# Neighbourhood attention: transposes of two steps issued together, values one turn later

## The chip, the cores and the metric

The kernel is one program on one core of a Trainium2 chip. The metric is the device time of one execution in microseconds (us), from the runs of the kernel before and of the changed kernel on the same chip. The engines are named as in the profile: PE (TensorE, matmuls; PEld its weight loads), DVE (VectorE), ACT (ScalarE), POOL (GpSimd), SP (SyncE, which issues DMAs).

## The reference

The reference is one layer of a hybrid encoder over 512 tokens of width 1024. After an RMS norm, one projection feeds three branches: a bidirectional mLSTM, a two-dimensional neighbourhood attention, and a cross-attention into 256 memory tokens. Each branch is projected back to width 1024, weighted by a sigmoid gate, summed, projected, and added to the input; a convolutional gated FFN and a final norm follow. The change lies in the neighbourhood attention alone (8 heads of 64, a grid of 8 rows by 64 columns, a window of 16 columns):

```python
s = jnp.einsum('bhrcd,bhrkjd->bhrckj', qg, k_band) * (NA_HEAD_DIM ** -0.5) + bias[None]
s = jnp.where(col_ok[None, None, None, :, None, :], s, -jnp.inf)
p = jax.nn.softmax(s.reshape(B, NA_HEADS, rows, GRID_W, kr * GRID_W), axis=-1).reshape(s.shape)
o = jnp.einsum('bhrckj,bhrkjd->bhrcd', p, v_band)
```

## The kernel before

Every float32 matrix product is made of three matmuls on two-part operands (`mm3`, L213 to L215: high by high, high by low, low by high). Weights come by DMA on SP's queue as raw blocks (`wr`) and are split into a high part `wh` by ACT (L195) and a low part `wl` by DVE (L196). There are four buffers each of `wh` and `wl`, so two blocks of two halves are held, and a split waits for PE to have read the block before the last.

The branches A, B and C are written as generators (`ml_all`, `na_all`, `xa_all`). The main code runs the dense projections and, between them, takes one turn of the generator at the head of a list with `step`. So PE gets a block of dense matmuls (24 of 512 columns, half of them for one output tile each where a block has two), then a few short matmuls of a branch, then the next block. The neighbourhood attention takes 18 such turns, t = 0 to 17, beside the gate projections (`gate`, drained by L1196 and L1197) and branch projections (drained by L1224 and L1225) of the second and third branch.

Its work is 16 steps i, one for each head and each half of the columns. A step has four stages:

- `scores(i)`: four matmuls of 256 columns (L944, L945) of zero-padded two-part queries (`QS`, `QZ`) with keys (`KS`) into one PSUM bank. DVE adds the bias and finds the maximum (L949), negates it (L951), ACT takes the exponential with row sums (L954), DVE the reciprocal (L955), ACT scales (L957). The result is the tile `sm`, shown as `s`.
- `transposes(i)`: four 128x128 transposes of `sm` on PE (L963) into one bank; ACT makes the high part (L970) and DVE the low part (L971) of two weight tiles `w`.
- `values(i)`: four matmuls of 256 columns (L982) of `w` with a window of values `vw`.
- `store(i)`: ACT and DVE add the parts and split the result (L994 to L1003) into `yh` and `yl`, which the third branch's projection reads after the last turn.

In turn t the kernel before issues `scores(t)`, then `values(t - 2)` and `store(t - 2)`, then `transposes(t - 1)`. `prep` (L920 to L924) makes queries and keys of the next pair of heads; it is called after the scores of turns 3, 7 and 11, and its instructions stand, as the scheduler placed them, in the odd turns. It writes the low part of the queries into `QZ`, of which there are two sets of two tiles, cleared once by POOL (L909). `load_vwin` issues 32 small DMAs on POOL's queue for the value window of a pair of heads, four steps ahead of its use.

A scheduler (the Tile layer) sets each engine's order from the order of the code, the free buffers and its own cost model; each engine then runs its list strictly in that order and waits at semaphores. The pools that matter here: four PSUM banks for scores, transposes and values (`at`), four for the dense products (`mm`), seven scratch tiles `s`, two `E` tiles for `w`, four `H` tiles.

Of the kernel before, what the change touches and what calls it, by code (L numbers as in the profile page):

```python
# [11 lines left out]
F32 = mybir.dt.float32  # L12
F32R = mybir.dt.float32r
# [4 lines left out]
P = 128  # L18
S = 512
# [91 lines left out]
def hybrid_block(ctx, tc, xg, xT, memT, wflat, vecs, gbias, nabias, outa, outb, outc):  # L111
    nc = tc.nc
    V, A, G, PE, SY = nc.vector, nc.scalar, nc.gpsimd, nc.tensor, nc.sync
# [5 lines left out]
    tp = ctx.enter_context(tc.tile_pool(name="tp", bufs=2))  # L119
# [6 lines left out]
    def nm(s):  # L126
        uid[0] += 1
        return f"{s}_{uid[0]}"

    def unit(dt=F32):  # L130
        return up.tile([P, UNIT], dt, tag="unit", name=nm("u"))

    def scr(n=512):
        return sp.tile([P, S], F32, tag="scr", name=nm("s"))[:, :n]

    def tiny(n):
        return tp.tile([P, 32], F32, tag="tiny", name=nm("y"), bufs=12)[:, :n]
# [4 lines left out]
    def atps():  # L142
        return atp.tile([P, 512], F32, tag="at", name=nm("at"))
# [144 lines left out]
    for i in range(2):  # L288
        t = cp.tile([P, 514], F32, name=f"pad{i}")
# [212 lines left out]
    for c in range(3):  # L502
        n, nk = TMC[c], TMK[c]
# [29 lines left out]
    def load_vwin(hp):  # L533

        vw = unit(F32R)
        for b in range(4):
            for hf in range(2):
                i = 2 * b + hf
                for r in range(4):
                    G.dma_start(vw[r * 32:(r + 1) * 32, i * 256:(i + 1) * 256],  # L540
                                nav_v[hf, r, CW[b]:CW[b] + 32, hp * 256:(hp + 1) * 256])
        return vw
# [360 lines left out]

    def na_all(nq, nk, vw0, yh, yl):

        QZ = [[tp.tile([P, S], F32R, tag="H", name=nm("QZ"), bufs=4) for _ in range(2)] for _ in range(2)]
        for pair in QZ:
            for e in range(2):
                G.memset(pair[e][64 - 64 * e:128 - 64 * e].bitcast(F32), 0.0)  # L909

        def prep(hp):
            qn = nq[:, hp * S:(hp + 1) * S]
            kn = nk[:, hp * S:(hp + 1) * S]
            QL = QZ[hp % 2]
            QS, KS = [], []
            for e in range(2):
                own, oth = slice(64 * e, 64 * e + 64), slice(64 - 64 * e, 128 - 64 * e)
                q2 = tp.tile([P, S], F32R, tag="R", name=nm("QS"), bufs=4)
                k2 = tp.tile([P, S], F32R, tag="R", name=nm("KS"), bufs=4)
                A.activation(q2[own], qn[own], AF.Copy)  # L920
                A.activation(k2[own], kn[own], AF.Copy)
                A.activation(q2[oth], qn[own], AF.Copy)
                V.tensor_tensor(k2[oth], kn[own], k2[own].bitcast(F32), op=ALU.subtract)
                V.tensor_tensor(QL[e][own], qn[own], q2[own].bitcast(F32), op=ALU.subtract)  # L924
                QS.append(q2)
                KS.append(k2.rearrange("p (r w) -> p r w", r=ROWS))
            return QS, KS, QL

        def bias_tile(i):
            bt = tp.tile([P, 2 * M], F32, tag="nab", name=nm("nab"))  # L930
            SY.dma_start(bt, nabias[i // 2, i % 2])
            return bt

        def scores(i, ops, bt):
            QS, KS, QL = ops
            e, bp = (i // 2) % 2, i % 2
            ps = atps()
            sm = scr()
            mx = tiny(2)
            for j in range(2):  # L940
                b = 2 * bp + j
                bs = slice(b * P, (b + 1) * P)
                ks = KS[e][:, :, CW[b]:CW[b] + 32]
                PE.matmul(ps[:, j * M:(j + 1) * M], QS[e][:, bs], ks, start=True, stop=False)  # L944
                PE.matmul(ps[:, j * M:(j + 1) * M], QL[e][:, bs], ks, start=False, stop=True)  # L945
            smv = sm.rearrange("p (a b) -> p a b", a=2)
            for j in range(2):
                js = slice(j * M, (j + 1) * M)
                V.tensor_tensor_reduce(smv[:, j, :], ps[:, js], bt[:, js], 1.0, 2.0 * NEG, ALU.add, ALU.max,  # L949
                                       accum_out=mx[:, j:j + 1])  # L950
            V.tensor_scalar(mx, mx, -1.0, None, op0=ALU.mult)  # L951
            su = tiny(2)
            for j in range(2):
                A.activation(smv[:, j, :], smv[:, j, :], AF.Exp, bias=mx[:, j:j + 1], accum_out=su[:, j:j + 1])  # L954
            V.reciprocal(su, su)  # L955
            for j in range(2):
                A.activation(smv[:, j, :], smv[:, j, :], AF.Copy, scale=su[:, j:j + 1])  # L957
            return sm

        def transposes(i, sm):  # L960
            pt = atps()
            for j in range(4):
                PE.transpose(pt[:, j * P:(j + 1) * P], sm[:, j * P:(j + 1) * P], ident)  # L963

            pp = []
            for bl in range(2):
                w = tp.tile([P, 4, P], F32R, tag="E", name=nm("w")).rearrange("p a b -> p (a b)")
                wv = w[:, :512].rearrange("p (k x q) -> p k x q", k=2, x=2)
                src = pt[:, bl * 256:(bl + 1) * 256].rearrange("p (k q) -> p k q", k=2)
                A.activation(wv[:, :, 0, :], src, AF.Copy)  # L970
                V.tensor_tensor(wv[:, :, 1, :], src, wv[:, :, 0, :].bitcast(F32), op=ALU.subtract)  # L971
                pp.append(w)
            return pp

        def values(i, pp, vw):

            e, bp = (i // 2) % 2, i % 2
            py = atps()
            for bl in range(2):
                for hf in range(2):  # L980
                    c = (2 * (2 * bp + bl) + hf) * 256 + e * P
                    PE.matmul(py[:, bl * 256:(bl + 1) * 256], vw[:, c:c + P], pp[bl][:, hf * 256:(hf + 1) * 256],  # L982
                              start=hf == 0, stop=hf == 1)
            return py

        def store(i, py):

            h, bp = i // 2, i % 2
            e = h % 2
            hs, es, os = slice(h // 2 * S, (h // 2 + 1) * S), slice(64 * e, 64 * e + 64), slice(64 - 64 * e, 128 - 64 * e)  # L990
            pv = py.rearrange("p (b x q) -> p b x q", b=2, x=2)
            y = scr(256)
            yv = y.rearrange("p (b q) -> p b q", b=2)
            A.activation(yv[es], pv[os, :, 0, :], AF.Copy)  # L994
            V.tensor_tensor(yv[es], yv[es], pv[es, :, 1, :], op=ALU.add)
            V.tensor_tensor(yv[es], yv[es], pv[es, :, 0, :], op=ALU.add)
            bs = slice(2 * bp, 2 * bp + 2)
            y4 = y[es].rearrange("p (b r c) -> p b r c", b=2, r=ROWS)
            yhv = yh[es, hs].rearrange("p (r b c) -> p b r c", r=ROWS, b=4)[:, bs]
            ylv = yl[es, hs].rearrange("p (r b c) -> p b r c", r=ROWS, b=4)[:, bs]  # L1000
            for b in range(2):
                A.activation(yhv[:, b], y4[:, b], AF.Copy)
                V.tensor_tensor(ylv[:, b], y4[:, b], yhv[:, b].bitcast(F32), op=ALU.subtract)  # L1003

        n = 16
        ops = prep(0)
        bt = bias_tile(0)
        sms, pts = {}, {}
        vws = {0: vw0}
        yield  # L1010
        for t in range(n + 2):
            if t < n:
                nb = bias_tile(t + 1) if t + 1 < n else None
                sms[t] = scores(t, ops, bt)
                bt = nb
                if t % 4 == 3 and t + 1 < n:
                    ops = prep((t + 1) // 4)
            i = t - 2
            if 0 <= i:
                if i % 4 == 0 and i + 4 < n:  # L1020
                    vws[i // 4 + 1] = load_vwin(i // 4 + 1)
                store(i, values(i, pts.pop(i), vws[i // 4]))
            i = t - 1
            if 0 <= i < n:
                pts[i] = transposes(i, sms.pop(i))
            yield


# [103 lines left out]
    for f in range(4):  # L1132
        ps = paced(("o", f), RN if f else RB)
        t = scr()
# [50 lines left out]
    for br in range(3):  # L1185
# [3 lines left out]
        if br == 1:  # L1189
            vw0 = load_vwin(0)  # L1190
            ys[2] = [unit(F32R), unit(F32R)]
            gens.append(na_all(nq, nk, vw0, *ys[2]))
            step(1)
# [360 lines left out]
```

## Time and profile before

| | |
|---|---|
| time, median of 3 runs | 873.18 us (872.92 to 873.79) |
| the profiled execution's own time | 873.18 us |
| its span, first to last instruction | 871.2 us |
| PE busy | 865.8 us, 99% of the span |
| DVE, ACT, POOL busy | 594.7, 467.8, 125.4 us (68%, 54%, 14%) |
| granted PE clock | 1.000 |
| turns of the neighbourhood attention | from 312.2 us to 427.5 us |

The first matmul row of a turn (L944) marks its start, and a start is more telling than a duration here: matmuls overlap in the array, a 512-column one is recorded with 0.39 us but the next starts 0.227 us later. The rows that the argument uses stand in the prediction.

### The profile page before, as it was taken

How to read it: one execution, taken by the hardware profiler on the slowest of the kernel's cores; microseconds unless marked ns; L12 is line 12 of the kernel's file. 1: busy time of each engine (PE TensorE's matmuls, PEld its weight loads, DVE VectorE, ACT ScalarE, POOL GpSimd, SP SyncE). 2: the span in 40 equal slices, each digit the busy share in tenths (PEclk: the TensorE clock that was granted, in tenths of full speed). 3: DMA queues.
4: the chain of work that ended last, by engine and by line, in shares of the span. 5: the costliest groups of instructions: out<-in, count | busy, mean ns of one | idle time of the engine just before them, and what ended most of it. 6: DMA issues, size and time to landing. Idle time of an engine off the chain costs nothing.

```text
span 871.2 us, 12230 instructions
## 1 busy us (share of the span) xinstructions
PE 865.8 (99%) x4287; PEld 733.9 (84%) x4287; DVE 594.7 (68%) x1292; ACT 467.8 (54%) x981; POOL 125.4 (14%) x202
## 2 busy tenths in 40 slices
PE   9999999999999999999999999999999999999997
PEld 7898889888888888888888888888888888888887
DVE  7794698997477768897676558776633466666534
ACT  7563577764355658897534455444422344444532
POOL 0101100000344370600000002111100011111010
PEclk9999999999999999999999999999999999999999
DMA  8324643533343453533223433323233323232412
GB/s 281 101 75 147 196 140 89 169 107 115 93 132 82 113 146 112 160 116 122 99 96 109 144 109 97 98 96 98 78 98 113 102 96 97 96 98 87 141 35 97
DMA packets 39421, 99.81 MB, mean 115 GB/s; under 512 B 5688, under 2 KB 13880, under 8 KB 39360
## 3 DMA queue, kind: packets, MB, share of 16 engines
q1 hardware_dynamic: 31568, 92.32, 32.6%
q0 software_dynamic: 7360, 6.32, 3.4%
q8 instruction: 34, 0.56, 0.3%
q10 hardware_dynamic: 432, 0.39, 0.1%
q14 instruction: 27, 0.22, 0.1%
HBM read 94.80 MB, written 4.21 MB: 114 GB/s over the span
## 4 chain that ended last, share of the span: by engine, by line
PE 98%; DVE 1%; issue 0%; ACT 0%; POOL 0%; POOLq 0%
PE mm L213 29%; PE mm L215 29%; PE mm L214 29%; PE at L214 2%; PE at L213 2%; PE at L215 2%; PE at L982 1%; PE at L963 1%; PE at L944 0%; PE at L945 0%; PE at L765 0%; PE at L813 0%; PE at L1070 0%; PE at L243 0%; PE mm L422 0%
## 5 line engine op out<-in xcount | busy, mean ns | idle before, releaser
L213 PE MATMUL mm<-u,wh 128*128 128x512 f32 (+1 forms) x1072 | 414.3, 386 | 0.0
L215 PE MATMUL mm<-u,wl 128*128 128x512 f32 (+1 forms) x1072 | 411.8, 384 | 0.0
L214 PE MATMUL mm<-u,wh 128*128 128x512 f32 (+1 forms) x1072 | 411.5, 384 | 0.0
L195 ACT ACTIVATE wh<-wr 128x512 fp32r<-128x512 f32 (+2 forms) x298 | 184.2, 621 | 219.9 <-PE mm L214 177.2
L196 DVE TENSOR_TENSOR wl<-wr,wh 128x512 fp32r<-128x512 f32 (+3 forms) x300 | 203.4, 681 | 88.5 <-ACT wh L195 86.4
L215 PEld LDWEIGHTS mm<-u,wl 128*128 128x128 f32 x1072 | 201.3, 188 | 40.3 <-DVE wl L196 0.4
L213 PEld LDWEIGHTS mm<-u,wh 128*128 128x128 f32 x1072 | 201.5, 188 | 39.0 <-ACT wh L195 0.4
L214 PEld LDWEIGHTS mm<-u,wh 128*128 128x128 f32 x1072 | 201.5, 188 | 38.5
L1418 POOL TENSOR_TENSOR s<-s,rb 128x512 f32<-128x512 f32 x22 | 38.2, 1736 | 401.7 <-DVE s L1417 238.9
L540 POOL DMA_DIRECT2D u<-nav_d x128 | 62.5, 535 | 70.5 <-DVE X L220 24.3
L219 ACT ACTIVATE u<-s 128x512 fp32r<-128x512 f32 x26 | 16.4, 632 | 56.4 <-DVE s L1421 56.3
L1421 DVE TENSOR_TENSOR s<-mm,s 128x512 f32<-128x512 f32 x22 | 15.2, 690 | 23.9 <-POOL s L1418 23.9
L460 ACT ACTIVATE s<-pad,vec 128x512 f32<-128x512 f32 x30 | 24.4, 813 | 9.7 <-DVE pad L458 9.7
L220 DVE SCALAR_TENSOR_TENSOR u<-s,u 128x512 fp32r<-128x512 f32 x26 | 19.1, 733 | 14.8 <-ACT u L219 14.5
L461 DVE SCALAR_TENSOR_TENSOR s<-pad,vec,s 128x512 f32<-128x512 f32 x30 | 22.5, 750 | 5.5 <-ACT s L460 5.5
L1417 DVE SCALAR_TENSOR_TENSOR s<-s,s 128x512 f32<-128x512 f32 x22 | 15.2, 691 | 13.4 <-ACT s L1416 13.3
L462 DVE SCALAR_TENSOR_TENSOR s<-pad,vec,s 128x512 f32<-128x512 f32 x30 | 22.5, 750 | 0.9
L1416 ACT ACTIVATE s<-s 128x512 f32<-128x512 f32 x22 | 13.9, 632 | 14.9 <-DVE s L1415 14.9
L1196 DVE TENSOR_TENSOR s<-mm,rb_x 128x512 f32<-128x512 f32 x16 | 11.0, 689 | 13.8 <-PE mm L215 13.7
L458 DVE TENSOR_TENSOR pad<-mm,rb 128x512 f32<-128x512 f32 x22 | 15.1, 690 | 6.4 <-PE mm L215 6.2
L1428 DVE TENSOR_TENSOR u<-mm,u 128x512 f32<-128x512 f32 x13 | 9.0, 692 | 14.6 <-PE mm L215 14.6
L214 PE MATMUL mm<-wl,u 128*128 128x512 f32 x48 | 18.7, 390 | 0.0
(352 smaller groups left out, 1053.3 us busy)
## 6 DMA issues: line engine op xcount, KB each, us to landing
wr<-wflat SPq DMA_DIRECT2D x141, 512.0 KB, 3.3
nab<-nabias SPq DMA_DIRECT2D x16, 256.0 KB, 2.7
u<-nav_d POOLq DMA_DIRECT2D x128, 32.0 KB, 2.8
s<-xT SPq DMA_DIRECT2D x15, 256.0 KB, 4.0
wr<-wflat SPq DMA_DIRECT2D x14, 192.0 KB, 2.4
nav_d<-nv POOLq DMA_DIRECT2D x8, 256.0 KB, 2.5
R<-rd SPq DMA_DIRECT2D x8, 256.0 KB, 4.6
wr<-wflat SPq DMA_DIRECT2D x2, 544.0 KB, 3.4
```

The lines of the kernel that those rows point to most:

```text
L195: A.activation(h[:, u:v], src, AF.Copy)
L196: V.tensor_tensor(l[:, u:v], src, h[:, u:v].bitcast(F32), op=ALU.subtract)
L213: PE.matmul(ps, lh, rh, start=start, stop=False)
L214: PE.matmul(ps, lh, rl, start=False, stop=False)
L215: st["mm"] = PE.matmul(ps, ll, rh, start=False, stop=stop).ins
L219: A.activation(h, src, AF.Copy, scale=scale)
L220: V.scalar_tensor_tensor(l, src, scale, h.bitcast(F32), op0=ALU.mult, op1=ALU.subtract)
L460: A.activation(t1, pad[:, 0:512], AF.Identity, scale=vcol(w, i), bias=vcol(b, i))
L461: V.scalar_tensor_tensor(t1, pad[:, 1:513], vcol(w, n + i), t1, op0=ALU.mult, op1=ALU.add)
L462: V.scalar_tensor_tensor(t1, pad[:, 2:514], vcol(w, 2 * n + i), t1, op0=ALU.mult, op1=ALU.add)
L540: G.dma_start(vw[r * 32:(r + 1) * 32, i * 256:(i + 1) * 256], nav_v[hf, r, CW[b]:CW[b] + 32, hp * 256:(hp + 1) * 256])
L1418: G.tensor_tensor(c, c, rb2, op=ALU.mult)
```

## The change

In turn t the changed code issues `values` and `store` of step t - 3 first, then the transposes, then `scores(t)`. Transposes are issued in odd turns only, of the two steps t - 2 and t - 1 (step 0 alone in turn 1, step 15 alone in turn 16); in turn 17 the values of steps 14 and 15 come together. The weight tiles of odd steps now have two tiles of their own (`odd`, of the pool `H`), those of even steps stay in the pool `E`. To free the two `H` tiles there is one set of zero-padded low queries (`QL`) in place of two, with half of the clearing on POOL.

```diff
-        QZ = [[tp.tile([P, S], F32R, tag="H", name=nm("QZ"), bufs=4) for _ in range(2)] for _ in range(2)]
-        for pair in QZ:
-            for e in range(2):
-                G.memset(pair[e][64 - 64 * e:128 - 64 * e].bitcast(F32), 0.0)
+        QL, odd = [[tp.tile([P, S], F32R, tag="H", name=nm(n), bufs=4) for _ in range(2)] for n in ("QZ", "w")]
+        for e in range(2):
+            G.memset(QL[e][64 - 64 * e:128 - 64 * e].bitcast(F32), 0.0)
...
-            QL = QZ[hp % 2]
...
-                w = tp.tile([P, 4, P], F32R, tag="E", name=nm("w")).rearrange("p a b -> p (a b)")
+                if i % 2:
+                    w = odd[bl]
+                else:
+                    w = tp.tile([P, 4, P], F32R, tag="E", name=nm("w")).rearrange("p a b -> p (a b)")
...
         for t in range(n + 2):
+            for i in range(max(0, t - 3), t - 2 + (t == n + 1)):
+                if i % 4 == 0 and i + 4 < n:
+                    vws[i // 4 + 1] = load_vwin(i // 4 + 1)
+                store(i, values(i, pts.pop(i), vws[i // 4]))
+            if t % 2 or t == n:
+                for i in range(max(0, t - 2 + (t == n)), t):
+                    if i in sms:
+                        pts[i] = transposes(i, sms.pop(i))
             if t < n:
                 nb = bias_tile(t + 1) if t + 1 < n else None
                 sms[t] = scores(t, ops, bt)
                 bt = nb
                 if t % 4 == 3 and t + 1 < n:
                     ops = prep((t + 1) // 4)
-            i = t - 2
-            if 0 <= i:
-                if i % 4 == 0 and i + 4 < n:
-                    vws[i // 4 + 1] = load_vwin(i // 4 + 1)
-                store(i, values(i, pts.pop(i), vws[i // 4]))
-            i = t - 1
-            if 0 <= i < n:
-                pts[i] = transposes(i, sms.pop(i))
             yield
```

The code below the change keeps its text; line numbers of the changed kernel differ by one or two (L944 becomes L942, L963 becomes L961, L982 becomes L983, L949 becomes L947, L955 becomes L953, L971 becomes L972). PE keeps the same instructions in the same number.

PE's order at turn 9, between two dense blocks (`mm` tiles), before:

```order
L215 MATMUL mm_4236<-u_149,wl_4150 128x512
L944 MATMUL at_4265<-KS_4106,QS_4105 128x256
L945 MATMUL at_4265<-KS_4106,QZ_3418 128x256
L944 MATMUL at_4265<-KS_4106,QS_4105 128x256
L945 MATMUL at_4265<-KS_4106,QZ_3418 128x256
L982 MATMUL at_4281<-w_4219,u_3623 128x256 x2
L982 MATMUL at_4281<-w_4222,u_3623 128x256 x2
L963 MATMUL at_4294<-ident,s_4186 128x128 x4
L213 MATMUL mm_4316<-u_147,wh_4228 128x512
```

The same turn in the changed kernel (`s_4178` is the softmax of step 8, `s_4093` that of step 7):

```order
L215 MATMUL mm_4204<-u_149,wl_4129 128x512
L983 MATMUL at_4231<-w_4084,u_3659 128x256 x2
L983 MATMUL at_4231<-w_4087,u_3659 128x256 x2
L961 MATMUL at_4244<-ident,s_4093 128x128 x4
L961 MATMUL at_4253<-ident,s_4178 128x128 x4
L942 MATMUL at_4266<-KS_4109,QS_4108 128x256
L943 MATMUL at_4266<-KS_4109,QZ_3418 128x256
L942 MATMUL at_4266<-KS_4109,QS_4108 128x256
L943 MATMUL at_4266<-KS_4109,QZ_3418 128x256
L213 MATMUL mm_4293<-u_147,wh_4196 128x512
```

The scores moved from the front of the group to its end, and two sets of transposes stand side by side; the even turns beside it hold only values and scores.

DVE's order in turn 8, from the first part of step 8's scores (`s_4186`) to the reciprocal of its row sums, before:

```order
L949 ISA s_4186,y_4187<-at_4185,nab_4087 128x256
L949 ISA y_4187 128x1
L1225 TENSOR_TENSOR u_2709<-u_2709,s_4049 128x512
L949 ISA s_4186,y_4187<-at_4185,nab_4087 128x256
L949 ISA y_4187 128x1
L995 TENSOR_TENSOR s_4206<-s_4206,at_4201 64x256
L951 TENSOR_SCALAR y_4187<-y_4187 128x2
L971 TENSOR_TENSOR w_4219<-at_4214,w_4219 128x2x128
L996 TENSOR_TENSOR s_4206<-s_4206,at_4201 64x256
L196 TENSOR_TENSOR wl_4229<-wr_4050,wh_4228 128x512
L955 RECIPROCAL y_4195<-y_4195 128x2
```

The same stretch in the changed kernel (step 8's scores are `s_4178`, its reciprocal the last row):

```order
L947 ISA s_4178,y_4179<-at_4177,nab_4090 128x256
L947 ISA y_4179 128x1
L997 TENSOR_TENSOR s_4167<-s_4167,at_4162 64x256
L947 ISA s_4178,y_4179<-at_4177,nab_4090 128x256
L947 ISA y_4179 128x1
L196 TENSOR_TENSOR wl_4201<-wr_3987,wh_4200 128x512
L1004 TENSOR_TENSOR u_3417<-s_4167,u_3416 64x8x16 x2
L949 TENSOR_SCALAR y_4179<-y_4179 128x2
L196 TENSOR_TENSOR wl_4286<-wr_4122,wh_4285 128x512
L953 RECIPROCAL y_4187<-y_4187 128x2
```

No low part of a transposed weight tile (L971 before) stands in this even turn any more; the store of an earlier step (L997, L1004) and two splits of dense weights (L196) stand ahead of the reciprocal, and of the splits only one comes between the negated maximum (L949 now) and the reciprocal.

## The prediction

> **What bounds the kernel now.** I read the page first, then who PE waits for, then the turns of the neighbourhood attention by windows, then single rows. The page's busy times and its chain that ended last:
>
> ```profile
> span 871.2 us, 12230 instructions
> ...
> PE 865.8 (99%) x4287; PEld 733.9 (84%) x4287; DVE 594.7 (68%) x1292; ACT 467.8 (54%) x981; POOL 125.4 (14%) x202
> ...
> PE 98%; DVE 1%; issue 0%; ACT 0%; POOL 0%; POOLq 0%
> ```
>
> PE is the chain: 98% of it. The view of waits for PE has one row in the whole execution, at the first matmul:
>
> ```profile
> PE at L243 <- PEq L1541: 0.8, 1, 0.8
> ```
>
> So in the stage of the change PE never waits, and there are two ways to another time: PE's own instructions take less or more, or something is late that was in time. Windows by turn (columns: length; busy us and instructions of PE, PEld, DVE, ACT, POOL; granted clock; DMA share; GB/s), turns 7, 8, 9 and 14:
>
> ```profile
> 358.82:365.68 6.86, 6.86 (x37) 5.90 (x36) 5.82 (x17) 6.70 (x17) 4.81 (x10) 1.00 0.58 157
> 365.68:372.55 6.87, 6.87 (x37) 5.90 (x36) 6.64 (x19) 4.77 (x14) 0.03 (x1) 1.00 0.19 51
> 372.55:379.42 6.87, 6.87 (x38) 5.90 (x36) 6.45 (x18) 6.43 (x17) 0.00 (x0) 1.00 0.62 194
> ...
> 406.88:413.75 6.87, 6.87 (x37) 5.90 (x36) 4.80 (x15) 5.09 (x15) 0.00 (x0) 1.00 0.23 78
> ```
>
> All turns last the same 6.87 us at full clock, whether DVE has 4.80 or 6.64 us of work in them. In turns 7 to 9 DVE and ACT are nearly as full as PE; that is where lateness would begin.
>
> **What PE pays for each kind of group.** PE's timeline (start, duration), turns 0, 1, 2, 4 and the end of 17:
>
> ```profile
> 312.16 0.28 PE L944 MATMUL at<-KS,QS 128*128 128x256 f32 x1
> ...
> 312.64 0.39 PE L213 MATMUL mm<-u,wh 128*128 128x512 f32 x1
> ...
> 318.08 0.28 PE L944 MATMUL at<-KS,QS 128*128 128x256 f32 x1
> ...
> 324.48 0.28 PE L944 MATMUL at<-KS,QS 128*128 128x256 f32 x1
> ...
> 338.22 0.28 PE L944 MATMUL at<-KS,QS 128*128 128x256 f32 x1
> ...
> 338.70 0.64 PE L982 MATMUL at<-w,u 128*128 128x256 f32 x4
> 339.17 0.60 PE L963 MATMUL at<-ident,s 128*128 128x128 f32 x4
> 339.53 0.48 PE L213 MATMUL mm<-u,wh 128*128 128x512 f32 x1
> 339.85 0.39 PE L214 MATMUL mm<-u,wh 128*128 128x512 f32 x1
> 340.08 0.40 PE L215 MATMUL mm<-u,wl 128*128 128x512 f32 x1
> ...
> 345.08 0.28 PE L944 MATMUL at<-KS,QS 128*128 128x256 f32 x1
> ```
>
> Turn 0 has 24 dense matmuls, from 312.64 to 318.08: 5.44 us, 0.227 each. Before them stand the four scores, 0.48 us. Turn 1 (scores, transposes, 24 dense) lasts 6.40 us against 5.92 for turn 0, so a set of four transposes costs 0.48 (0.473 before rounding of the starts). Turn 4 lasts 6.86, so a group of four values adds 0.47. The costs add up; there is no large price for changing kind.
>
> How much of the 0.473 is hand-over? One transpose is recorded with 0.272 us, four together with 0.60 (339.17):
>
> ```profile
> L963 PE MATMUL at<-ident,s x64: 270/272/276, 318.6 to 421.4; 128*128 128x128 f32 x64
> ```
>
> So three intervals take 0.60 - 0.27 = 0.33, one 0.109, and four transposes 0.437. What is left, 0.473 - 0.437 = 0.036 us, is the hand-over: the first dense matmul after them begins while the last transpose still runs and the second comes only 0.32 later (339.53 to 339.85), the third after 0.23.
>
> **The change, part by part.**
>
> *Fewer hand-overs.* The instructions of PE stay; their groups change. 16 sets of transposes become 7 pairs and 2 singles, so 7 hand-overs go: 7 x 0.036 = 0.25 us gained, all of it on the path, since PE is the path. The trace has no two sets side by side and no scores behind transposes. Bounds: if all 16 hand-overs vanish, because scores now stand between transposes and the dense block, 16 x 0.036 = 0.6 us gained; if a short score pays for the transposes the 0.09 us that the first dense matmul shows above 0.227 (0.32), in each of 9 places, 0.8 us lost. I take 0.25, nearest to the measured set.
>
> The Trainium skill, page "TensorE: Matmul & The Clock Gate", section "Back-to-back issue gap", gives for sustained pairs of weight load and matmul about 81 ns at 128 columns and about 131 ns at 512. By it a second set of four could take 0.32 instead of 0.437, an estimate of 7 x 0.11 = 0.8 us more gain, 872.2 in all. The rows disagree with the skill at the long end (0.227 measured, 0.131 stated) and show 0.109 at the short end, so the sum goes by the rows.
>
> *Values one turn later, scores last.* Nothing is added on PE. The transposes of an even step come earlier against PE's work: ahead of those of step 8 stand one group of scores (0.48) and one of values (0.47) fewer than before. This is the one place where cover shrinks. Step 8's softmax on DVE and ACT, and its transposes (turn 9):
>
> ```profile
> 369.14 0.17 DVE L951 TENSOR_SCALAR y<-y 128x2 f32<-128x2 f32 x1
> 369.34 0.42 DVE L971 TENSOR_TENSOR w<-at,w 128x256 fp32r<-128x256 f32 x1
> 369.80 0.42 DVE L996 TENSOR_TENSOR s<-s,at 64x256 f32<-64x256 f32 x1
> 370.25 0.69 DVE L196 TENSOR_TENSOR wl<-wr,wh 128x512 fp32r<-128x512 f32 x1
> 370.86 0.16 DVE L955 RECIPROCAL y<-y 128x2 f32<-128x2 f32 x1
> ...
> 369.34 0.51 ACT L954 ACTIVATE s<-s,y 128x256 f32<-128x256 f32 x1 [1.62 <-DVE y L951]
> ...
> 370.25 0.19 ACT L954 ACTIVATION_READ_ACCUMULATOR s<-s,y 128x1 f32 x1
> ...
> 371.40 0.91 ACT L957 ACTIVATE s<-s,y 128x256 f32<-128x256 f32 x2
> ...
> 373.50 0.60 PE L963 MATMUL at<-ident,s 128*128 128x128 f32 x4
> ```
>
> It is ready at 371.40 + 0.91 = 372.31, 1.19 us before PE takes it, the shortest margin of the even steps. After: PE comes at 373.50 - 0.95 - 0.11 (three hand-overs gone by then) = 372.44. DVE: from the reciprocal of step 0 to that of step 8 the changed list has two more L196 (2 x 0.69), and one each of L971, L995, L996 fewer (3 x 0.42): 0.12 more. Between L951 and the reciprocal two items fewer (L971, L996) now hide the exponentials; these need 1.3 us (from 369.14 to the end of the second read at 370.44), the one L196 left covers 0.69. So L951 comes at about 369.14 + 0.12 + 0.84 = 370.1, the reciprocal at 371.5 and the softmax at 371.5 + 0.2 + 0.91 = 372.6. PE waits about 0.15 us there. Steps 2, 6, 12 and 14 have an L1224 and L1225 or a set of L971, L995 and L996 less ahead of their reciprocals, and more margin to begin with; I put them, with 4 and 10, at no wait. What a wait holds up: everything behind it on PE, since PE takes its list in order; so it is paid in full.
>
> *Transposed weights.* Those of odd steps are read one turn after they are made, as before; the tightest place is in the second half of step 6's (DVE, then PE's second pair 0.23 behind the row's start):
>
> ```profile
> 365.75 0.41 DVE L971 TENSOR_TENSOR w<-at,w 128x256 fp32r<-128x256 f32 x1
> ...
> 366.17 0.64 PE L982 MATMUL at<-w,u 128*128 128x256 f32 x4
> ```
>
> Ready at 366.16, read at 366.40. In the changed order an even step's weights have a turn more (over 6 us); an odd step's are split first in their turn and gain the scores that now stand behind them. The added L971 of the pair lies beside PE's dense block. No cost. Weight splits (`wh`, `wl`) that slip behind the pair are covered by the two-block buffers: ACT's splits spend their time waiting for PE, not the reverse:
>
> ```profile
> L195 ACT ACTIVATE wh<-wr 128x512 fp32r<-128x512 f32 (+2 forms) x298 | 184.2, 621 | 219.9 <-PE mm L214 177.2
> ```
>
> *One query set, other queues.* The low queries are written by L924 after the same DVE list has used the scores that read them, so one set adds no wait; the two clearings that go are POOL's, of 0.52 us each and 80 us ahead of the first scores:
>
> ```profile
> L909 POOL MEMSET QZ<- x4: 518/520/523, 187.5 to 232.1; 64x512 f32 x4
> L540 POOL DMA_DIRECT2D u<-nav_d x32: 492/499/557, 346.5 to 365.2; - x32
> ```
>
> The last value window (32 DMAs, second row) waits for values of an earlier window, so it may begin a turn later, near 353, and be in by 375; its first values come in turn 15, after 406.88. SP's bias tiles swap places with a weight block, and each is issued a turn (6.4 us at least) ahead of its scores; the page shows 2.7 us to landing:
>
> ```profile
> nab<-nabias SPq DMA_DIRECT2D x16, 256.0 KB, 2.7
> ```
>
> After turn 17 two gate blocks (10.9 us of dense work) still stand before the third branch's projection and cover two stores instead of one.
>
> **Sum.** 873.18 - 0.25 + 0.15 = 873.1 us. The profiled execution's 873.18 is 1.98 more than its span and equals the median of the runs. A change of 0.2% (1.75 us) is about what a measurement of this kernel can tell from none.
>
> **Rivals.**
> - *Softmaxes late (slower).* In the odd turns DVE gets both splits of a pair and half of `prep`; turns 8 and 9 have 6.64 and 6.45 us of DVE in 6.87, so a backlog of an odd turn has nowhere to go before the next transposes. If one L196 more (0.69) comes ahead at steps 4, 8 and 10, which all lie beside or just behind branch projections, that is 2.1 us and 875.2. It decides from 2.0 us of waits in all. Against it: the DVE work ahead of each reciprocal grows by no more than 0.12 us, and the later steps (turn 14: 4.80 us) have room.
> - *Nothing saved.* The hand-over costs the same into scores, and small waits stay: 873.2 to 874.8.
> - *A real gain (faster).* It takes 1.75 us. If the second set ran at the dense pace (0.227 / 4 = 0.057 for 128 columns) instead of 0.109, 28 transposes would give 1.5 and the hand-overs 0.25: 871.4. Against it: within a set the later transposes already follow without a break, and show 0.109.
>
> **How the numbers follow.** Forecast (hand-overs saved, waits under 0.4 us): 0.62, own range 872.4 to 873.6. Nothing saved or small waits: 0.21. Softmaxes late by 2 us or more: 0.12. Real gain: 0.05. Faster 0.05, within 0.2% 0.83, slower 0.12. The range leaves out the real gain and most of the large waits, and takes in, below, both gains together (0.25 and 0.6) and the 0.3 us by which the lowest run (872.92) lies under the median, and above, two steps that wait 0.9 us each with nothing saved: 872.0 to 874.9.
>
> **What would show it.** Right: turns of the changed kernel near 6.4 us (even) and 7.3 us (odd) that sum to 13.7 per pair; eight transposes in 0.87 us; no PE wait but some 0.1 us at turn 9. Wrong: rows of PE waiting for ACT's L955 at L961 in several odd turns, for DVE at L983, or transposes closer than 0.109.

## The result: slower by 0.27%, and the profile after

The changed kernel took 875.69 us (median of 10 runs, 875.38 to 876.16), the kernel before 873.27 us (10 runs, 872.79 to 873.93) on the same chip. The ratio is 1.0027 with an interval of 1.0017 to 1.0037. The forecast was 873.1, range 872.0 to 874.9: the time lies above the range. Two executions among the experiments, one of 1245 us (*scores between*) and one of 3116 us (*tiles only*), were far slower than the others of their kernels and are left out of the medians below.

The page of the changed kernel, the lines that answer to those of before (span, busy time by engine, the chain that ended last by engine):

```profile
span 873.9 us, 12233 instructions
...
PE 867.7 (99%) x4287; PEld 733.8 (84%) x4287; DVE 595.9 (68%) x1292; ACT 467.6 (54%) x981; POOL 123.5 (14%) x200
...
PE 93%; DVE 3%; ACT 2%; issue 1%; POOL 0%; POOLq 0%; DVEq 0%
```

PE is still 99% busy by the records, but the chain is PE for 93% only. DVE and ACT together now hold 5% of it. The view of waits for PE names the place: transposes that wait for the scaling of the softmax.

```profile
PE at L961 <- ACT s L955: 0.7, 1, 0.7
```

This view shows only gaps that reach past the modelled end of the matmul before. To see all that was lost I use one stretch that holds the same instructions in every kernel: from the first scores of turn 0 to the end of the nineteen dense blocks that start there. In windows of that stretch (columns as in the prediction: length, then busy us and instructions of PE, PEld, DVE, ACT, POOL), the kernel before and the changed one:

```profile
312.16:438.36 126.20, 126.20 (x649) 107.88 (x648) 99.91 (x273) 97.97 (x247) 26.24 (x54) 1.00 0.42 128
```

```profile
312.59:441.05 128.46, 127.67 (x649) 107.79 (x648) 99.94 (x273) 97.04 (x247) 26.13 (x54) 1.00 0.42 126
```

128.46 - 126.20 = 2.26 us, of 2.42 between the medians. So nearly the whole loss is in the turns of the neighbourhood attention. Below, "the stage" is this stretch. Turns 7, 8, 9, 11 and 16 of the changed kernel:

```profile
358.23:365.81 7.58, 7.58 (x42) 6.31 (x40) 6.43 (x19) 6.62 (x16) 5.16 (x11) 1.00 0.65 165
365.81:372.21 6.40, 6.40 (x33) 5.47 (x32) 6.37 (x18) 4.37 (x13) 4.84 (x10) 1.00 0.40 99
372.21:380.62 8.41, 7.73 (x41) 6.31 (x40) 6.55 (x19) 7.56 (x20) 0.00 (x0) 1.00 0.47 152
...
387.03:394.86 7.83, 7.72 (x41) 6.30 (x40) 7.35 (x21) 6.39 (x17) 0.00 (x0) 1.00 0.22 69
...
422.41:429.19 6.78, 6.78 (x33) 5.41 (x32) 4.00 (x10) 4.19 (x11) 0.00 (x0) 1.00 0.23 77
```

Even turns last 6.40 or 6.41 us, all of them. An odd turn without a wait lasts 7.32 (turns 9 and 11 of a later experiment, *stores after the scores*, show it). Turns 7, 9 and 11 last 7.58, 8.41 and 7.83, so they wait 0.26, 1.09 and 0.51 us. Turn 16 lasts 6.78 where it takes 6.38 in the experiment *no scaling*, without a wait: 0.40 us. Turn 15, with 7.42, adds 0.1. The sum is 2.36 us of waits, and 0.10 us is gained elsewhere in the stage.

**The chain of step 8.** PE, DVE and ACT of the changed kernel in turns 7 to 9 (start, duration, idle time before it and what ended it):

```profile
361.48 0.43 DVE L972 TENSOR_TENSOR w<-at,w 128x256 fp32r<-128x256 f32 x1 [0.42 <-ACT w L971]
...
362.82 0.42 DVE L972 TENSOR_TENSOR w<-at,w 128x256 fp32r<-128x256 f32 x1 [0.26 <-ACT w L971]
...
363.97 0.41 DVE L947 CUSTOM_DVE_ANT_0 s<-at,nab 128x256 f32<-128x256 f32 x1
...
366.64 0.29 PE L943 MATMUL at<-KS,QZ 128*128 128x256 f32 x1
...
367.01 0.16 DVE L953 RECIPROCAL y<-y 128x2 f32<-128x2 f32 x1
...
368.33 0.68 DVE L196 TENSOR_TENSOR wl<-wr,wh 128x512 fp32r<-128x512 f32 x1
...
369.54 0.40 DVE L996 TENSOR_TENSOR s<-s,at 64x256 f32<-64x256 f32 x1
369.87 0.41 DVE L947 CUSTOM_DVE_ANT_0 s<-at,nab 128x256 f32<-128x256 f32 x1
...
370.89 0.68 DVE L196 TENSOR_TENSOR wl<-wr,wh 128x512 fp32r<-128x512 f32 x1
...
371.89 0.15 DVE L949 TENSOR_SCALAR y<-y 128x2 f32<-128x2 f32 x1
...
373.21 0.17 DVE L953 RECIPROCAL y<-y 128x2 f32<-128x2 f32 x1 [0.57 <-ACT s L952]
...
373.41 0.91 ACT L955 ACTIVATE s<-s,y 128x256 f32<-128x256 f32 x2 [0.23 <-DVE y L953]
...
372.69 0.60 PE L961 MATMUL at<-ident,s 128*128 128x128 f32 x4
373.97 0.84 PE L961 MATMUL at<-ident,s 128*128 128x128 f32 x4 [0.68 <-ACT s L955]
```

The scores of step 8 are done on PE at 366.93 (366.64 + 0.29). DVE touches them first at 369.87, 2.9 us later. Until then it works off other things: the drains of a branch projection, a split of weights, and L996, the store of an earlier step. Between the two parts of the bias stands L997, behind them another split and two L1004. The softmax is done at 373.41 + 0.91 = 374.32. PE is ready for it at 372.69 + 4 x 0.11 = 373.13. Already in turn 7 the same happened: the bias of step 7 begins at 363.97, behind the four splits of the pair (L972), two of which wait for ACT. In the kernel before, step 7's reciprocal stood here:

```profile
363.27 0.17 DVE L955 RECIPROCAL y<-y 128x2 f32<-128x2 f32 x1 [0.65 <-ACT s L954]
```

So step 7's reciprocal came at 363.27 before and at 367.01 now, step 8's at 370.86 and 373.21. (0.43 us of each difference is only the start of the stage, 312.59 for 312.16.)

**The wait of turn 11** has another face. DVE and ACT in turn 10:

```profile
382.96 0.42 DVE L947 CUSTOM_DVE_ANT_0 s<-at,nab 128x256 f32<-128x256 f32 x1
...
384.03 0.42 DVE L996 TENSOR_TENSOR s<-s,at 64x256 f32<-64x256 f32 x1 [0.64 <-ACT s L995]
384.49 0.43 DVE L947 CUSTOM_DVE_ANT_0 s<-at,nab 128x256 f32<-128x256 f32 x1
...
382.88 0.71 ACT L1198 ACTIVATE s<-s,mgbh 128x512 f32<-128x512 f32 x1
383.62 0.38 ACT L995 ACTIVATE s<-at 64x256 f32<-64x256 f32 x1
385.41 0.51 ACT L1003 ACTIVATE u<-s 64x128 fp32r<-64x128 f32 x2 [1.41 <-DVE s L997]
385.94 0.51 ACT L952 ACTIVATE s<-s,y 128x256 f32<-128x256 f32 x1
```

L996 belongs to the store of step 7. It stands between the two parts of step 10's bias and waits 0.64 us for ACT's L995, which stands behind the gate's tanh (L1198). The second part of the bias stands behind it and waits too. Then the store's copies (L1003) go ahead of the exponentials (L952) on ACT.

### The profile page after: what moved, and what is told of

Its sections match the earlier page's. It is cut to its first block, busy times and chain, and to the rows that moved or that the text cites. A ratio compares the mean times of both kernels' runs of the same rounds, so it can differ in the third digit from the quotient of the medians.

```text
span 873.9 us, 12233 instructions
## 1 busy us (share of the span) xinstructions
PE 867.7 (99%) x4287; PEld 733.8 (84%) x4287; DVE 595.9 (68%) x1292; ACT 467.6 (54%) x981; POOL 123.5 (14%) x200
## 4 chain that ended last, share of the span: by engine, by line
PE 93%; DVE 3%; ACT 2%; issue 1%; POOL 0%; POOLq 0%; DVEq 0%
PE mm L215 28%; PE mm L213 28%; PE mm L214 28%; PE at L214 2%; PE at L213 2%; PE at L215 2%; PE at L961 1%; PE at L983 1%; ACT s L955 1%; DVE s L947 0%; PE at L765 0%; PE at L813 0%; PE at L1071 0%; ACT s L952 0%; PE at L243 0%
## 5 line engine op out<-in xcount | busy, mean ns | idle before, releaser
L196 DVE TENSOR_TENSOR wl<-wr,wh 128x512 fp32r<-128x512 f32 (+3 forms) x300 | 204.7, 685 | 87.7 <-ACT wh L195 85.6
L952 ACT ACTIVATE s<-s,y 128x256 f32<-128x256 f32 x32 | 16.0, 501 | 9.4 <-DVE y L949 9.2
```

The source lines that it names most:

```text
L196: V.tensor_tensor(l[:, u:v], src, h[:, u:v].bitcast(F32), op=ALU.subtract)
```

## The experiments

Two theories stood at the start. A: PE comes to the transposes of an even step 0.95 us earlier, and its softmax isn't ready by then. B: the burst of work that a pair makes in one turn on DVE and ACT delays everything. C to F came with the runs and are told in their expectations. All edits are to the changed kernel unless it is said otherwise. The time of before is that of runs on the same chip.

| kernel | time, us | before, us | ratio (interval) | stage, us |
|---|---|---|---|---|
| before | 873.27 | | | 126.20 |
| changed | 875.69 | 873.27 | 1.0027 (1.0017 to 1.0037) | 128.46 |
| stores after the scores | 873.49 | 873.48 | 1.0000 (0.9991 to 1.0009) | 126.31 |
| scores first | 873.49 | 873.45 | 1.0001 (0.9992 to 1.0009) | 126.32 |
| scores between | 876.07 | 873.48 | 1.0030 (1.0018 to 1.0042) | 128.83 |
| unpaired | 876.41 | 873.45 | 1.0035 (1.0021 to 1.0048) | 129.24 |
| pairs a turn later | 873.00 | 873.36 | 0.9995 (0.9986 to 1.0004) | 126.02 |
| unpaired, a turn later | 873.42 | 873.36 | 1.0002 (0.9993 to 1.0011) | 126.31 |
| no scaling | 873.32 | 873.48 | 0.9998 (0.9989 to 1.0007) | 126.10 |
| longer softmax | 878.04 | 873.45 | 1.0051 (1.0037 to 1.0065) | 130.44 |
| adds left out | 874.13 | 873.36 | 1.0010 (1.0001 to 1.0019) | 127.27 |
| adds on POOL | 876.59 | 873.45 | 1.0031 (1.0020 to 1.0043) | 129.64 |
| tiles only (on before) | 873.23 | 873.36 | 0.9999 (0.9989 to 1.0008) | |

### Which part of the change costs: order or pairing

*Scores first*: the pairs and the later values stay, the scores go back to the front of their turn.

```diff
         for t in range(n + 2):
+            if t < n:
+                ... scores(t) and prep, as below
             for i in range(max(0, t - 3), t - 2 + (t == n + 1)):
                 store(i, values(i, pts.pop(i), vws[i // 4]))
             if t % 2 or t == n:
                 ... transposes
-            if t < n:
-                ... scores(t) and prep
```

> The changed kernel with the scores at the front of each turn again (scores of t, values of t-3, then the pair of transposes); pairs, tiles and values a turn later stay. Theory A (the even step's transposes came 0.95 us earlier against its softmax, and PE waits for that): the waits of turns 7 to 16, 2.6 us in the changed kernel, go but for 0.3 at most, and the time is 873.0 to 873.3. Theory B (the double set of weight splits in odd turns makes DVE and ACT late, whatever the order on PE): the waits stay, 875.3 to 875.9.

Measured: 873.49, the stage 126.32, no wait. *Unpaired*: values and scores in the changed order, but transposes of one step in every turn.

```diff
-            if t % 2 or t == n:
-                for i in range(max(0, t - 2 + (t == n)), t):
-                    if i in sms:
-                        pts[i] = transposes(i, sms.pop(i))
+            i = t - 1
+            if 0 <= i < n:
+                pts[i] = transposes(i, sms.pop(i))
```

> The changed kernel without pairing: each turn takes values of t-3, transposes of t-1, scores of t. Theory A: every step's transposes, odd ones too, stand 0.95 us earlier than before the change, so PE waits in the turns where DVE is full (7 to 11), one us or more in all, 874.3 to 877. Theory B: no double set of splits, no waits, 873.0 to 873.4.

Measured: 876.41, the stage 129.24; turns 4, 6, 9, 10 and 12 wait, turn 12 by 1.04 us (it lasts 7.88, an undisturbed one 6.84). So the loss comes with the order "values, transposes, scores" and not with the pairs. But this order changes two things at once: PE comes to the transposes 0.95 us earlier against the scores, and in the code the store of the values stands ahead of the scores, so the scheduler puts its work on DVE and ACT ahead of the softmax. The next two runs part them.

### PE's part or DVE's: the two halves of the order

*Stores after the scores*: PE's order of groups stays that of the changed kernel; only the store is written behind the scores.

```diff
+            outs = []
             for i in range(max(0, t - 3), t - 2 + (t == n + 1)):
-                store(i, values(i, pts.pop(i), vws[i // 4]))
+                outs.append((i, values(i, pts.pop(i), vws[i // 4])))
             ... transposes, then scores(t) and prep
+            for i, ps in outs:
+                store(i, ps)
```

> The changed kernel with PE's order unchanged, but the stores of a turn (L994 to L1004 on ACT and DVE) written after its scores, so that on DVE and ACT they stand behind the bias and maximum of these scores and not ahead of them or between them. Theory F (the softmax is late because the store of an earlier step and what it waits for stand ahead of it in DVE's list): step 8's negated maximum comes 1.2 us earlier, the waits at turns 7, 9 and 11 go, under 0.4 us of waits in all; the stage takes 126.0 to 126.3 us against 128.5 in the changed kernel and 126.2 before; 872.9 to 873.3. Rival A (the 0.95 us that PE comes earlier decide alone, whatever DVE's order): waits over 2 us stay, 875.2 to 875.7.

Measured: 873.49 against 873.48, the stage 126.31. Turns 9 and 11 both last 7.32. Turn 9 in a window, then DVE and PE for step 8 (the first row is step 7's reciprocal):

```profile
372.11:379.43 7.32, 7.32 (x42) 6.34 (x41) 6.25 (x19) 6.74 (x18) 0.00 (x0) 1.00 0.54 183
```

```profile
366.00 0.15 DVE L953 RECIPROCAL y<-y 128x2 f32<-128x2 f32 x1
...
368.60 0.41 DVE L947 CUSTOM_DVE_ANT_0 s<-at,nab 128x256 f32<-128x256 f32 x1
...
368.94 0.41 DVE L947 CUSTOM_DVE_ANT_0 s<-at,nab 128x256 f32<-128x256 f32 x1
...
369.29 0.41 DVE L996 TENSOR_TENSOR s<-s,at 64x256 f32<-64x256 f32 x1
369.62 0.15 DVE L949 TENSOR_SCALAR y<-y 128x2 f32<-128x2 f32 x1
369.69 0.68 DVE L196 TENSOR_TENSOR wl<-wr,wh 128x512 fp32r<-128x512 f32 x1
...
370.62 0.68 DVE L196 TENSOR_TENSOR wl<-wr,wh 128x512 fp32r<-128x512 f32 x1
371.22 0.15 DVE L953 RECIPROCAL y<-y 128x2 f32<-128x2 f32 x1
...
372.58 1.04 PE L961 MATMUL at<-ident,s 128*128 128x128 f32 x8
```

The two parts of the bias now follow each other, the negated maximum is there at 369.62 in place of 371.89 (the turn begins 0.10 us earlier), and eight transposes run without a break. Of the waits only 0.2 us at turn 16 is left. With the order of groups on PE unchanged, the order of DVE's and ACT's lists alone took away the loss. With these lists there is room for PE's 0.95 us: the rival falls.

Theory F, that it is the store which stands ahead, holds in part. In turn 7 the store stood ahead of step 7's bias and now stands behind it; step 7's reciprocal comes at 366.00 in place of 367.01. In turn 10 L996 no longer stands between the two parts of the bias. But from step 7's reciprocal to step 8's negated maximum both lists hold four instructions of stores (L996, L997, two L1004). What is gone from there are two weight splits (L196, at 368.33 and 370.89 in the changed kernel), which the scheduler placed anew, behind the maximum, when the store was moved; the stretch shrinks from 4.88 to 3.62 us. No run parts the splits from the store.

*Scores between*: the store stays ahead, PE gets half of the 0.95 us back.

```diff
             ... values and store
+            if t < n:
+                ... scores(t) and prep
             if t % 2 or t == n:
                 ... transposes
-            if t < n:
-                ... scores(t) and prep
```

> The changed kernel with the scores of a turn between its values and its transposes: PE reaches the transposes 0.48 us later, half of the 0.95, and the stores still stand ahead of the softmax. Every wait of a step should shrink by up to 0.48 us: turn 9 from 1.13 to about 0.65, turn 11 from 0.55 to 0.1, turn 7 to nothing, turn 16 (no scores there) stays 0.4; the stage 127.4, the time 874.2. If the waits were set by PE alone and not by a fixed lateness of the softmax, they would not shrink so: 875.2 or more.

Measured: 876.07, a miss. The transposes waited even less than expected: 0.1 us in turn 9, and nothing in turns 7, 11, 15 and 16. But new waits came at the values: 0.4 us each in turns 4 and 10, and in turn 12 0.56 ahead of the first pair of them and 1.2 behind it. PE at turns 11 and 12:

```profile
387.29 1.04 PE L961 MATMUL at<-ident,s 128*128 128x128 f32 x8
...
394.20 0.59 PE L983 MATMUL at<-w,u 128*128 128x256 f32 x2 [0.42 <-ACT s L952]
395.48 0.56 PE L983 MATMUL at<-w,u 128*128 128x256 f32 x2 [0.69 <-DVE w L972]
```

Here the values of step 9 wait for the low part of its weights (L972), which come from transposes that now stand last in turn 11 (what ended the idle time of the first row, 0.42 us put down to the exponentials, isn't settled). In turn 8 DVE's list from the split at 368.33 to the reciprocal is that of the changed kernel. The softmax of step 8 ends 6.90 us after its scores are done on PE, for 7.39 in the changed kernel, and PE comes 0.48 later; together they take all but 0.1 us of that wait away. So the loss at the transposes needs both halves, an earlier PE and a later softmax. What the expectation overlooked is who then stands behind: the weights of the transposes that were moved to the end came too late for the values.

### Room of one more turn

*Pairs a turn later*: the pairs move to even turns, of steps t - 3 and t - 2, values follow.

```diff
-        for t in range(n + 2):
-            for i in range(max(0, t - 3), t - 2 + (t == n + 1)):
+        for t in range(n + 3):
+            for i in range(max(0, t - 4), t - 3 + (t == n + 2)):
...
-            if t % 2 or t == n:
-                for i in range(max(0, t - 2 + (t == n)), t):
+            if t % 2 == 0 or t == n + 1:
+                for i in range(max(0, t - 3 + (t == n + 1)), t - 1):
```

> The changed kernel with the pairs of transposes and the values each one turn later (pairs now in even turns, of steps t - 3 and t - 2, so the later step of a pair has a full dense block more). Theory A (the softmax of the later step of a pair is late on DVE and ACT, nothing else): no wait of PE at L961, turns 6.41 and 7.31 us, 13.72 for two against 13.73 before, time 0.1 us below the kernel before: 873.2. Rival B (the burst of four splits and of the stores in one turn itself delays the chain): waits of 1 to 2.5 us stay, 874.5 to 875.7.

*Unpaired, a turn later*:

```diff
-        for t in range(n + 2):
-            for i in range(max(0, t - 3), t - 2 + (t == n + 1)):
+        for t in range(n + 3):
+            for i in range(max(0, t - 3), t - 2):
...
-            if t % 2 or t == n:
-                for i in range(max(0, t - 2 + (t == n)), t):
-                    if i in sms:
-                        pts[i] = transposes(i, sms.pop(i))
+            i = t - 2
+            if 0 <= i < n:
+                pts[i] = transposes(i, sms.pop(i))
```

> As the kernel with transposes unpaired, but transposes a turn later (of step t - 2) and values with them (t - 3): each turn values, four transposes, scores. Theory A: no wait, and the turns keep the 6.84 us of the undisturbed turns of the unpaired kernel against 6.867 before, 16 x 0.025 = 0.4 us gained: 872.9. Rival (what is gained comes from pairing the transposes): turns of 6.867, 873.3.

Measured: 873.00 and 873.42. No wait in either, so the burst of four splits in one turn doesn't by itself make PE wait. The stage of the first and two of its turns, in windows:

```profile
311.92:437.94 126.02, 126.02 (x649) 107.86 (x648) 99.22 (x273) 97.20 (x247) 26.26 (x54) 1.00 0.43 128
363.56:370.88 7.32, 7.32 (x41) 6.33 (x40) 7.31 (x21) 4.64 (x14) 0.00 (x0) 1.00 0.22 73
370.88:377.29 6.41, 6.41 (x34) 5.46 (x32) 4.42 (x14) 6.31 (x17) 0.00 (x0) 1.00 0.51 157
```

The paired one has the shortest stage of all, 0.18 us below before and 0.29 below its unpaired sister (126.31). In the time this can't be told from no change (0.9986 to 1.0004), so it beats neither the kernel before nor what can be measured.

### The length of the chain and the load of DVE

*No scaling* leaves out the reciprocal and the scaling of the softmax (the weights aren't normalized):

```diff
-            V.reciprocal(su, su)
-            for j in range(2):
-                A.activation(smv[:, j, :], smv[:, j, :], AF.Copy, scale=su[:, j:j + 1])
```

> The changed kernel without reciprocal and scaling of the softmax (L953 and L955 are left out, so the weights are not normalized): the chain ends about 1.1 us earlier (0.2 and 0.9). All theories by which the softmax is late: no wait over 0.1 us at turns 7, 11, 15 and 16, at most 0.1 at turn 9, stage 126.0 to 126.2, time 873.0 to 873.2. If PE's grouping itself cost time (hand-overs, PSUM banks), the stage would stay above 127.

Measured: 873.32, the stage 126.10, no wait. *Longer softmax* adds two copies on ACT to each even step:

```diff
+            if i % 2 == 0:
+                for j in range(2):
+                    A.activation(smv[:, j, :], smv[:, j, :], AF.Copy)
```

> The changed kernel with two more ACT copies of 0.45 us behind the softmax of each even step (work added, same result). Theory A: the chain to the transposes grows by 0.9 us in each pair; turns 7, 9, 11, 13, 15 are at or over their margin and grow by 0.8 to 0.9 each, turn 5 (margin 0.1) too, turns 1 and 3 (margins 1.2 and 1.5) not: 4.5 to 5.4 us more than the changed kernel, 880 to 881. Theory C (PE itself is slower with the new groups): 875.5 to 876, since ACT has room.

Measured: 878.04, the stage 130.44, about half of the loss that was expected; turns 5, 7, 9, 11, 13 and 15 wait 0.4 to 0.7 us each. Turn 9 waits less than in the changed kernel (0.7 against 1.1), since the lists are others again. Both runs say that the end of the softmax ends the wait; neither says why it is late.

*Adds left out* takes eight adds of the second branch (L1226) from DVE (that branch is then missing from the sum):

```diff
-                    V.tensor_tensor(mgv(f), mgv(f), tg[i], op=ALU.add)
+                    if br != 1:
+                        V.tensor_tensor(mgv(f), mgv(f), tg[i], op=ALU.add)
```

> The changed kernel without the second branch's adds into the merged sum (L1226, 8 adds of 0.68 us on DVE in turns 1 to 11 or so; that part of the output is left out). Theory C (DVE comes to the scores of the even steps with a backlog of other work): the wait at turn 9 falls from 1.13 to under 0.2 us, that at turn 11 below 0.3, all waits together from 2.6 to under 1.2: 874.0 to 874.4. Rival D (the length of the chain from DVE to ACT and back, whatever stands ahead of it): waits over 2 us stay, 875.2 to 875.7.

Measured: 874.13, the stage 127.27. Turn 9 lasts 7.42, a wait of 0.1 in place of 1.09: two of these adds stood ahead of step 8's bias. Turn 11 lasts 8.04, a wait of 0.72, more than the 0.51 of the changed kernel: the store still stands ahead of step 10's softmax on DVE and ACT. So theory C holds for turn 9 and fails for turn 11.

*Adds on POOL* was meant to do the same with the adds kept:

```diff
-                    V.tensor_tensor(mgv(f), mgv(f), tg[i], op=ALU.add)
+                    (G if br == 1 else V).tensor_tensor(mgv(f), mgv(f), tg[i], op=ALU.add)
```

> The changed kernel with the eight additions into the merged sum in the second branch (L1226, 0.6 us each on DVE) on POOL. If DVE's queue makes the softmaxes late: 0.6 to 1.2 us less ahead of those of steps 4, 8 and 10, the waits of turns 9 and 11 (1.1 and 0.55) shrink to 0.3 or less together, those of 13, 15 and 16 stay: 874.2 to 874.8. If the chain from score to scaled row is itself too long for the gap: 875.3 to 875.9.

Measured: 876.59, the stage 129.64, a miss for every theory. DVE was held up by POOL itself (last section), and the wait of turn 9 grew to 2.0 us (it lasts 9.34 for 7.32). It tells nothing about the load of DVE.

### The tiles

*Tiles only*: the kernel before with one set of low queries and own weight tiles of odd steps, and its own order.

```diff
-        QZ = [[tp.tile([P, S], F32R, tag="H", name=nm("QZ"), bufs=4) for _ in range(2)] for _ in range(2)]
+        QL, odd = [[tp.tile([P, S], F32R, tag="H", name=nm(n), bufs=4) for _ in range(2)] for n in ("QZ", "w")]
...
-                w = tp.tile([P, 4, P], F32R, tag="E", name=nm("w")).rearrange("p a b -> p (a b)")
+                if i % 2:
+                    w = odd[bl]
+                else:
+                    w = tp.tile([P, 4, P], F32R, tag="E", name=nm("w")).rearrange("p a b -> p (a b)")
```

> The kernel before with one set of zero-padded queries and own weight tiles of odd steps, its order of stages unchanged. All theories: nothing waits for these tiles, turns of 6.87 us, the same time as before within 0.3 us, 873.0 to 873.6. If the tiles cost something, waits of DVE or ACT for them show at L970 to L972 and PE's turns grow.

Measured: 873.23 against 873.36, ratio 0.9999 (0.9989 to 1.0008). Whether DVE or ACT waits at L970 to L972 isn't shown. The tiles and the query set cost nothing in the time.

## Why the prediction was wrong

**The step that failed is "Values one turn later, scores last", at the arrival of step 8's softmax.** It put the negated maximum at 370.1, the softmax at 372.6, and a wait of 0.15 us. The rows show 371.89, 374.32, and 1.09 us; 0.43 us of the first two differences is the later start of the stage. Counted from the end of step 8's scores on PE (before 366.05 + 0.28 = 366.33, now 366.93), the transposes followed after 7.17 us before (at 373.50) and the softmax was done after 5.98 (372.31), a margin of 1.19. Now PE is there after 6.20 (at 373.13) and the softmax after 7.39. So PE's order took 0.97 us of the margin, as forecast, and would by itself have left 0.2; the softmax took 1.41, where the forecast had about 0.4 (372.6 for 372.31, and the scores 0.11 earlier).

The forecast worked with DVE's busy time: 0.12 us more work from the reciprocal of step 0 to that of step 8. That sum was right to 0.4 us. Windows between these two reciprocals, before and after (the third busy time after the length is DVE's):

```profile
315.57:370.86 55.29, 55.29 (x289) 47.39 (x288) 47.24 (x129) 45.60 (x117) 22.99 (x48) 1.00 0.49 146
```

```profile
316.07:373.21 57.14, 57.14 (x296) 48.60 (x294) 46.95 (x129) 44.99 (x114) 23.02 (x48) 1.00 0.51 144
```

DVE has 46.95 us of work in place of 47.24, yet takes 57.14 us in place of 55.29: it stood idle for 10.19 us and not 8.05. An engine that runs a list in order loses time where the item at its head isn't ready. Who it waited for in the changed kernel and before:

```profile
DVE y L953 <- ACT s L952: 3.7, 4, 1.2
...
DVE w L972 <- ACT w L971: 1.2, 4, 0.4
```

```profile
DVE y L955 <- ACT s L954: 2.7, 4, 1.2
...
DVE w L971 <- ACT w L970: 0.3, 1, 0.3
```

DVE's waits for exponentials grew by 1.0 us and those for the high parts of the weights by 0.9. But idle time isn't the whole of it. The same stretch with the stores after the scores:

```profile
316.15:371.22 55.07, 55.07 (x285) 47.11 (x284) 45.58 (x125) 44.00 (x112) 23.12 (x48) 1.00 0.49 144
```

It is 2.07 us shorter than in the changed kernel: 0.70 is less idle time (9.49 us), and 1.37 is work that stands behind the reciprocal there, one split and two L1004 for the most part. So the arrival depends on both, what waits in the list and what is placed ahead. The prediction looked for waits of PE only, and gave DVE's work a cover in sums. It had seen in the list that L997 and L1004 stand ahead of the reciprocal now, but not that L996 comes between or ahead of the two parts of the bias and depends on ACT's list.

Its other points:

- *The steps put at no wait.* Steps 2, 4 and 12 held. Steps 6, 10 and 14 waited 0.26, 0.51 and 0.1 us at turns 7, 11 and 15, step 15 waited 0.40 at turn 16. "More margin to begin with" was taken from the shape of the DVE list, without going through a single chain.
- *Fewer hand-overs.* 0.25 us were forecast; without waits the stage shows 0.10 (no scaling) to 0.18 (pairs a turn later) below before. A turn with a pair and one without take 7.32 + 6.41 = 13.73 us in most places, as much as two turns of before; three of the turns with a pair in *pairs a turn later* last 7.27, which is 0.05 less. So there is a gain at about half the forecast, if it is one: each figure is from one profiled execution. That it comes from pairing fits 126.02 against 126.31 for the unpaired sister, but a pair with the scores first (126.32) has none of it.
- *PE's rows.* Even turns near 6.4 are right. Odd turns without a wait last 7.32 for 7.3. Eight transposes are recorded with 1.04 us, (1.04 - 0.27) / 7 = 0.110 each, for 0.109. The Trainium skill ("TensorE: Matmul & The Clock Gate", section "Back-to-back issue gap") gives 81 ns for each of a stream of pairs of weight load and matmul at 128 columns; the two sets here don't reach it, and the estimate of 872.2 worked out from that sentence (873.1 - 0.8 is 872.3) falls with it.
- *Transposed weights, query set, queues at no cost.* Right in the changed kernel: no row of PE waits for weight tiles, and the tiles alone measure a ratio of 0.9999. But it holds only for this order: with the scores between, the same weights came 0.69 us late.
- *The rival "Softmaxes late"* is what happened. It named the crowd of splits and `prep` in odd turns as the cause and 2.1 us, 875.2, as the price; the waits are 2.36 us, and steps 8 and 10 are among those that it named. It had been given 0.12, on the sum of busy time. The experiments add what it lacked: beside the splits, the store of an earlier step stands ahead of the softmax, in turn 10 between its two parts. In turn 8 itself the lists of the changed kernel and of *stores after the scores* differ by two weight splits, the kind of item that the rival had priced; which of the two decides for step 8 wasn't parted.

What stays open: turn 16 waits 0.40 us in the changed kernel and 0.2 with the stores behind. And the list with the stores behind also moved two weight splits; a kernel in which only the store or only the splits move wasn't run.

## What to carry to other kernels

When code is moved on a full engine, ask in what order the *other* engines will then serve its helpers: here the new order of groups on PE took most of a margin, the new lists of DVE and ACT took more than the rest, and writing the stores a few lines later gave back the whole loss. The arrival of a chain on in-order engines can't be had from sums of busy time; follow the chain row by row in the new lists, with each item's own supplier, and count an item that waits in front of a ready one as a delay of both. A quarter of a microsecond in a whole stage isn't worth a microsecond of margin.

## What the runs showed of the hardware

An add on POOL with both operands in SBUF holds up an operation of DVE that reads two SBUF operands. In the kernel with the adds on POOL, DVE and POOL in turns 8 and 11:

```profile
371.13 0.41 DVE L947 CUSTOM_DVE_ANT_0 s<-at,nab 128x256 f32<-128x256 f32 x1
...
388.82 1.17 DVE L196 TENSOR_TENSOR wl<-wr,wh 128x512 fp32r<-128x512 f32 x1 [0.31 <-ACT wh L195]
```

```profile
370.48 1.31 POOL L1226 TENSOR_TENSOR u<-u,s 128x512 f32<-128x512 f32 x1
...
388.08 1.37 POOL L1226 TENSOR_TENSOR u<-u,s 128x512 f32<-128x512 f32 x1 [14.86 <-DVE s L1225]
```

The split L196, of 0.68 us elsewhere, took 1.17 and ended 0.54 us after POOL's add (388.82 + 1.17 = 389.99; 388.08 + 1.37 = 389.45): it ran when POOL was done. L947, with one operand in PSUM, ran beside another add in its usual 0.41. The longest such split, in turn 8, is recorded with 2.45 us from 367.15 and also ended 0.55 us after an add, of 367.74 to 369.05; its record begins 0.59 us ahead of that add, and what held it until then isn't shown. The Trainium skill ("GPSIMD Engine Reference", section "8. Key points") names such contention for DVE instructions with two SBUF inputs; these rows agree.
